# One GpSimd queue for loads and stores, with the last load behind the first store, in a rotary embedding kernel

## The chip, the cores and the metric

The kernel runs on one core of a Trainium2 chip. The metric is device time in microseconds (us). A profiled execution also gives a span, which is about 1.8 us shorter than the device time. All ratios are those of the same rounds on the same chip: the mean time of one kernel's fast runs over that of the other's. They are not quite the ratios of the medians, which are quoted beside them.

## The reference

```python
x: (8, 8, 1024, 64) float32, scale = 0.5
angles = np.outer(positions * scale, freqs)
cos, sin = np.cos(angles), np.sin(angles)
x_first, x_second = x[..., :32], x[..., 32:]
out_first  = x_first * cos - x_second * sin
out_second = x_first * sin + x_second * cos
return np.concatenate([out_first, out_second], axis=-1)
```

Each element is read once and written once: 16.8 MB in and 16.8 MB out, with little arithmetic.

## The kernel before

The 64 heads are cut into four units of 16. A unit is a tile of 128 partitions with 8192 elements each, 4.19 MB of float32 in memory. A load casts to fp16 on the way in; in this kernel all loads with a cast are issued by GpSimd. VectorE multiplies and adds in fp16. ScalarE casts the result to float32 in an output buffer, and a store brings it back. Half of unit 0 is loaded without a cast, by SyncE and ScalarE, so that work starts early.

```python
    xin = ctx.enter_context(tc.tile_pool(name="xin", bufs=1))     # one X tile for each unit
    xout = ctx.enter_context(tc.tile_pool(name="xout", bufs=3))   # output buffers (and X0f)
    ...
    pin(nc.gpsimd.dma_start(out=Xf[0][:, :NH], in_=xv[0][:, :NH]))
    ...                                        # small constants on GpSimd
    for u in range(1, NU):
        pin(nc.gpsimd.dma_start(out=Xf[u], in_=xv[u]))
    ...                                        # sine and cosine tables T
    for u in range(NU):
        OUT = xout.tile([P, N], FP32, tag="O")
        for s in range(2):
            ...                                # four VectorE instructions on half a unit
            pin(nc.scalar.copy(out=OUT[:, ns], in_=Xf[u][:, ns]))
            if u in (0, NU - 1):
                pin(nc.sync.dma_start(out=ov[u][:, ns], in_=OUT[:, ns]))
        if u not in (0, NU - 1):
            pin(nc.gpsimd.dma_start(out=ov[u], in_=OUT))
```

`pin` keeps program order on each engine. So GpSimd's queue (q0 in the profile) held X0 half, X1, X2, X3, S1, S2, and SyncE's queue (q1) held S0a, S0b, S3a, S3b after a first load. X is a load, S a store, the figure is the unit, and a and b are its halves.

Of the kernel before, what the change touches and what calls it, by code (L numbers as in the profile page):

```python
# [21 lines left out]
def kernel(  # L22
# [8 lines left out]
    nc = tc.nc  # L31
    pin = tc.keep_in_program_order
# [9 lines left out]
    NU = NBH // HEADS  # L42
# [9 lines left out]
    xv = x.rearrange("b h s d -> (b h s d)").rearrange("(u p n) -> u p n", p=P, n=N)  # L52
    ov = out.rearrange("b h s d -> (b h s d)").rearrange("(u p n) -> u p n", p=P, n=N)
# [21 lines left out]
    Xf = [t.rearrange("p k h j -> p (k h j)") for t in X]  # L75
# [12 lines left out]
        out=one, in_=one, compare_op=ALU.not_equal, fill=1.0, base=0,  # L88
        pattern=[[-1, G], [-G, HP]], channel_multiplier=1,
    ))  # L90
    for u in range(1, NU):
        pin(nc.gpsimd.dma_start(out=Xf[u], in_=xv[u]))  # L92


# [6 lines left out]
        out=posf, in_=pos_i64.bitcast(I32).rearrange("p (k t) -> p k t", t=2)[:, :, 0]  # L101
# [3 lines left out]
        out=y,  # L105
# [8 lines left out]
        out=r, in0=m, scalar=_MAGIC, in1=y, op0=ALU.subtract, op1=ALU.subtract  # L114
# [5 lines left out]
        out=ra.bitcast(I32), in0=r.bitcast(I32), scalar1=0x7FFFFFFF, scalar2=None, op0=ALU.bitwise_and  # L120
# [5 lines left out]
    for g in range(0, G, 2):  # L126
        ps = spread.tile([P, 2, 2, W], FP32, tag="g")
        for i in range(2):
            nc.tensor.matmul(  # L129
                out=ps[:, i].rearrange("p t w -> p (t w)"),  # L130
# [9 lines left out]
    pin(nc.scalar.copy(out=Xf[0][:, NH:], in_=X0f[:, :NH]))  # L140


    for u in range(NU):
        OUT = xout.tile([P, N], FP32, tag="O")
        for s in range(2):
            ks = slice(s * KH, (s + 1) * KH)
            ns = slice(s * NH, (s + 1) * NH)
            Xs = X[u][:, ks]
            sin_b = T[:, 0, ks].unsqueeze(2).broadcast_to((P, KH, 2, half))
            cos_b = T[:, 1, ks].unsqueeze(2).broadcast_to((P, KH, 2, half))  # L150
            pr = tmp.tile([P, KH, 2, half], FP16, tag="pr")
            pin(nc.vector.tensor_tensor(out=pr, in0=Xs, in1=sin_b, op=ALU.mult))  # L152
            pin(nc.vector.tensor_tensor(out=Xs, in0=Xs, in1=cos_b, op=ALU.mult))  # L153
            pin(nc.vector.tensor_tensor(  # L154
                out=Xs[:, :, 0, :], in0=Xs[:, :, 0, :], in1=pr[:, :, 1, :], op=ALU.subtract
            ))
            pin(nc.vector.tensor_tensor(  # L157
                out=Xs[:, :, 1, :], in0=pr[:, :, 0, :], in1=Xs[:, :, 1, :], op=ALU.add
            ))
            pin(nc.scalar.copy(out=OUT[:, ns], in_=Xf[u][:, ns]))  # L160
            if u in (0, NU - 1):
                pin(nc.sync.dma_start(out=ov[u][:, ns], in_=OUT[:, ns]))
        if u not in (0, NU - 1):
            pin(nc.gpsimd.dma_start(out=ov[u], in_=OUT))  # L164
# [33 lines left out]
```

## Time and profile before

| | before |
|---|---|
| device time, median of 3 runs | 84.39 us (84.28 to 84.39) |
| span of the profiled run | 82.5 us |
| VectorE busy | 60.3 us, without a pause from 13.07 to 69.53 us |
| last store issued | 73.2 us |
| transfer engines, mean busy share from 1.7 to 81.3 us | 1.00 |
| moved in memory | 16.79 MB read, 16.78 MB written |

Two rows of the table are the ones to look at, that of VectorE and that of the transfer engines. VectorE is the busiest engine, but it ends 13 us before the span does. The 16 transfer engines ("DMA" in the profile) are never idle between the first load and the last store.

The DMA view of a stretch lists for each queue the packets, the MB and the busy share of the 16 engines. A packet of more than a few bytes is one row, that is, one partition's part of one transfer. The windows view gives for a stretch its bounds and length, then the busy time of PE, PEld, VectorE, ScalarE and GpSimd with instruction counts, the clock granted to TensorE, the DMA share and the GB/s. A cast load is counted there at its fp16 size, half of what it reads. Both views count a packet, with its whole time and all its bytes, in the stretch in which it starts, so that a share can come out a little above 1.

### The profile page before, as it was taken

The numbers are of one execution on the slowest core, as the hardware profiler recorded it, in microseconds if no ns is written. First come the engines' busy times: TensorE is split into PE (matmuls) and PEld (weight loads), VectorE is DVE, ScalarE is ACT, GpSimd is POOL, SyncE is SP. The second block draws the span as 40 slices with busy tenths as digits, with TensorE's granted clock in tenths as the row PEclk, the third lists the DMA queues.
The fourth block names the chain that finished last, engine by engine and source line by source line (L and its number), as shares of the span: only waits on it lengthen the run. The fifth ranks groups of instructions, "written<-read, shape, count | busy, mean of one in ns | idle before, by whom it ended". The sixth has DMA issues, their size and how long they took to land.

```text
span 82.5 us, 179 instructions
## 1 busy us (share of the span) xinstructions
PE 7.1 (9%) x18; PEld 2.8 (3%) x18; DVE 60.3 (73%) x40; ACT 40.1 (49%) x18; POOL 4.6 (6%) x14
## 2 busy tenths in 40 slices
PE   0020999200000000000000000000000000000000
PEld 0020333000000000000000000000000000000000
DVE  0306476999999999999999999999999997000000
ACT  0603069999950790393098059219606902940000
POOL 4920000000000000000000200000200000000000
PEclk9999999985555555555555555555555555555555
DMA  2899998997996999799979999996998999799990
GB/s 48 336 319 278 290 326 187 254 246 159 230 254 127 254 262 342 270 278 350 278 191 302 270 342 421 461 524 286 508 509 350 413 508 461 302 445 429 397 485 24
DMA packets 1874, 26.22 MB, mean 318 GB/s; under 512 B 338, under 2 KB 338, under 8 KB 338
## 3 DMA queue, kind: packets, MB, share of 16 engines
q0 software_dynamic: 864, 15.73, 66.2%
q1 hardware_dynamic: 720, 9.44, 27.5%
q10 hardware_dynamic: 290, 1.06, 3.3%
HBM read 16.79 MB, written 16.78 MB: 407 GB/s over the span
## 4 chain that ended last, share of the span: by engine, by line
DVE 55%; ACT 15%; issue 6%; DMA 5%; PE 5%; DVEq 1%; ACTq 0%
DVE X L153 20%; DVE pr L152 20%; DVE X L157 9%; DVE X L154 6%; DMA freq_row<-in_freqs_dram 5%; ACT T L139 5%; ACT OUT L160 4%; PE ps L129 4%; ACT X L140 4%; DVEq L193 1%; PE cfreq L97 1%; ACT tab L122 1%; DVE r L113 1%; DVE y L104 1%; ACTq L69 0%
## 5 line engine op out<-in xcount | busy, mean ns | idle before, releaser
L160 ACT CAST OUT<-X 128x4096 f32<-128x4096 f16 x8 | 28.9, 3607 | 24.2 <-DVE X L157 24.2
L152 DVE TENSOR_TENSOR pr<-X,T 128x4096 f16<-128x4096 f16 x8 | 18.3, 2292 | 1.0 <-ACT T L139 0.7
L153 DVE TENSOR_TENSOR X<-X,T 128x4096 f16<-128x4096 f16 x8 | 18.3, 2292 | 0.3
L154 DVE TENSOR_TENSOR X<-X,pr 128x2048 f16<-128x2048 f16 x8 | 9.8, 1225 | 0.3
L157 DVE TENSOR_TENSOR X<-pr,X 128x2048 f16<-128x2048 f16 x8 | 9.7, 1218 | 0.0
L139 ACT CAST T<-ps 128x1024 f16<-128x1024 f32 x6 | 5.7, 1028 | 2.6 <-PE ps L129 2.6
L129 PE MATMUL ps<-tab,sel 128*128 128x512 f16 x16 | 6.5, 599 | 2.2 <-ACT tab L122 2.2
L164 POOL DMA_DIRECT2D out_dram<-OUT x2 | 1.1, 538 | 54.1 <-ACT OUT L160 54.1
L137 DVE CAST T<-ps 128x1024 f16<-128x1024 f32 x2 | 2.5, 1225 | 2.2 <-PE ps L129 2.2
L140 ACT CAST X<-X0f 128x4096 f16<-128x4096 f32 x1 | 3.6, 3649 | 0.0
L95 DVE COPY sel<-one 128x2048 f16<-128x2048 f16 x1 | 0.7, 693 | 2.8 <-POOL one L87 2.8
L129 PEld LDWEIGHTS <-sel 128*128 128x128 f16 x16 | 2.3, 143 | 6.1 <-issue 6.1
L117 ACT ACTIVATE tab<-r 128x256 f16<-128x256 f32 x1 | 0.4, 418 | 4.1 <-DVE r L113 4.1
L117 ACT ACT_TABLE_LOAD x1 | 1.3, 1283 | 2.1 <-issue 2.1
L92 POOL DMA_DIRECT2D X<-in_x_dram x3 | 2.0, 658 | 0.0
L100 DVE CAST posf<-pos_i 128x8 f32<-128x8 int32 x1 | 0.2, 172 | 2.3 <-DMA pos_i<-in_positions_dram 2.3
L97 PE MATMUL cfreq<-freq_row,coef 1*128 1x32 f32 x2 | 0.6, 392 | 5.6 <-DMA freq_row<-in_freqs_dram 5.6
L83 POOL DMA_DIRECT2D X<-in_x_dram x1 | 0.7, 669 | 0.8 <-POOLq L179 0.8
L97 PEld LDWEIGHTS cfreq<-freq_row,coef 1*128 1x128 f32 x2 | 0.5, 306 | 5.6 <-issue 5.6
L104 DVE TENSOR_TENSOR y<-posf,cfreq 128x256 f32<-128x256 f32 x1 | 0.4, 422 | 0.3 <-PE cfreq L97 0.3
L122 ACT ACTIVATE tab<-ra,quarter 128x256 f16<-128x256 f32 x1 | 0.5, 507 | 0.0
L113 DVE SCALAR_TENSOR_TENSOR r<-m,y 128x256 f32<-128x256 f32 x1 | 0.4, 424 | 0.0
(10 smaller groups left out, 1.9 us busy)
## 6 DMA issues: line engine op xcount, KB each, us to landing
out_dram<-OUT SPq DMA_DIRECT2D x4, 2048.0 KB, 14.8
out_dram<-OUT POOLq DMA_DIRECT2D x2, 4096.0 KB, 15.3
X<-in_x_dram POOLq DMA_DIRECT2D x3, 2048.0 KB, 31.9
X0f<-in_x_dram SPq DMA_DIRECT2D x1, 1024.0 KB, 4.8
X<-in_x_dram POOLq DMA_DIRECT2D x1, 1024.0 KB, 11.7
X0f<-in_x_dram ACTq DMA_DIRECT2D x1, 1024.0 KB, 13.2
pos_i<-in_positions_dram ACTq DMA_DIRECT2D x1, 8.0 KB, 5.0
freq_row<-in_freqs_dram ACTq DMA_DIRECT2D x1, 0.1 KB
```

Source lines behind the costliest of these rows:

```text
L92: pin(nc.gpsimd.dma_start(out=Xf[u], in_=xv[u]))
L97: nc.tensor.matmul(out=cfreq, lhsT=coef, rhs=freq_row, start=True, stop=True)
L117: pin(nc.scalar.activation(out=tab[:, 0], in_=r, func=AF.Sin, bias=0.0, scale=-_TWO_PI_DN))
L129: nc.tensor.matmul(out=ps[:, i].rearrange("p t w -> p (t w)"), lhsT=sel[:, g + i].rearrange("s h q -> s (h q)"), rhs=tab.rearrange("s t k ...
L137: pin(nc.vector.tensor_copy(out=dst, in_=ps))
L139: pin(nc.scalar.copy(out=dst, in_=ps))
L140: pin(nc.scalar.copy(out=Xf[0][:, NH:], in_=X0f[:, :NH]))
L152: pin(nc.vector.tensor_tensor(out=pr, in0=Xs, in1=sin_b, op=ALU.mult))
L153: pin(nc.vector.tensor_tensor(out=Xs, in0=Xs, in1=cos_b, op=ALU.mult))
L154: pin(nc.vector.tensor_tensor(out=Xs[:, :, 0, :], in0=Xs[:, :, 0, :], in1=pr[:, :, 1, :], op=ALU.subtract))
L157: pin(nc.vector.tensor_tensor(out=Xs[:, :, 1, :], in0=pr[:, :, 0, :], in1=Xs[:, :, 1, :], op=ALU.add))
L160: pin(nc.scalar.copy(out=OUT[:, ns], in_=Xf[u][:, ns]))
```

## The change

The intent is to keep loads and stores apart and to bring each load no earlier than it is needed. All loads with a cast and the stores S0a, S0b, S1 and S2 go through one queue, in the order X0 half, X1, X2, S0a, X3, S0b, S1, S2. Only unit 3's stores stay on SyncE.

```diff
-    for u in range(1, NU):
+    for u in range(1, NU - 1):
         pin(nc.gpsimd.dma_start(out=Xf[u], in_=xv[u]))
 ...
             pin(nc.scalar.copy(out=OUT[:, ns], in_=Xf[u][:, ns]))
+            eng = nc.sync if u == NU - 1 else nc.gpsimd
             if u in (0, NU - 1):
-                pin(nc.sync.dma_start(out=ov[u][:, ns], in_=OUT[:, ns]))
+                pin(eng.dma_start(out=ov[u][:, ns], in_=OUT[:, ns]))
+            if (u, s) == (0, 0):
+                pin(eng.dma_start(out=Xf[NU - 1], in_=xv[NU - 1]))
```

## The prediction

> **What bounds the kernel now.** I write X0 to X3 for the loads of the four units and S0 to S3 for their stores; S0a and S0b are the two halves of a unit's store, and "X0 half" is the half of unit 0 that GpSimd loads. Every full unit is 4.19 MB in memory. I first read the page's busy line and the compute part of the timeline.
>
> ```profile
> PE 7.1 (9%) x18; PEld 2.8 (3%) x18; DVE 60.3 (73%) x40; ACT 40.1 (49%) x18; POOL 4.6 (6%) x14
> ```
> ```profile
> 13.07 2.29 DVE L152 TENSOR_TENSOR pr<-X,T 128x4096 f16<-128x4096 f16 x1 [0.67 <-ACT T L139]
> ...
> 45.27 0.54 POOL L164 DMA_DIRECT2D out_dram<-OUT  x1 [40.60 <-ACT OUT L160]
> ...
> 55.47 2.29 DVE L152 TENSOR_TENSOR pr<-X,T 128x4096 f16<-128x4096 f16 x1
> ...
> 59.37 0.53 POOL L164 DMA_DIRECT2D out_dram<-OUT  x1 [13.55 <-ACT OUT L160]
> ...
> 68.31 1.22 DVE L157 TENSOR_TENSOR X<-pr,X 128x2048 f16<-128x2048 f16 x1
> 69.56 3.61 ACT L160 CAST OUT<-X 128x4096 f32<-128x4096 f16 x1 [3.40 <-DVE X L157]
> ```
>
> The columns of the second fence are start, duration, engine, line, operation, and in brackets the idle time before it. VectorE runs from 13.07 to 69.53 us: eight halves at 2.29 + 2.29 + 1.22 + 1.22 us plus small gaps, near 7.05 us each. None of the idle time before its multiplies is put down to a load. ScalarE's last cast ends at 73.17 us and S3b, the last store, is issued then. That chain is fixed by the multiplies. The page's chain of waits ends with that cast and hides what follows: 9.3 us from 73.17 to the end of the 82.5 us span. So I next asked for the DMA share in three stretches (last two columns: DMA share and GB/s), and for the queues.
>
> ```profile
> 0.00:1.70 1.70, 0.00 (x0) 0.00 (x0) 0.00 (x0) 0.00 (x0) 0.65 (x5) 1.00 0.00 0
> 1.70:81.30 79.60, 7.14 (x18) 2.78 (x18) 60.31 (x40) 40.14 (x18) 3.98 (x10) 0.60 1.00 329
> 81.30:82.50 1.20, 0.00 (x0) 0.00 (x0) 0.00 (x0) 0.00 (x0) 0.00 (x0) 0.50 0.00 0
> ```
> ```profile
> q0 software_dynamic: 864, 15.73, 66.2%
> q1 hardware_dynamic: 720, 9.44, 27.5%
> q10 hardware_dynamic: 290, 1.06, 3.3%
> HBM read 16.79 MB, written 16.78 MB: 407 GB/s over the span
> ```
>
> This is the reading that matters: between 1.7 and 81.3 us the share is 1.00, so the transfer engines never run dry. The three queues are busy 66.2 + 27.5 + 3.3 = 97.0% of 82.5 us = 80.0 us, and 33.57 MB in 79.6 us is 422 GB/s. GB/s in the windows is lower because a load is counted at its fp16 size. The kernel is bound by transfers from end to end; the chain of multiplies is only just hidden behind them.
>
> Then I took the price of a row (one partition of one transfer), with the DMA view in short windows. Here the columns are packets, MB, share of 16 engines.
>
> Loads only, 15 to 22.6 us:
> ```profile
> q0 software_dynamic: 113, 1.59, 98.2%
> ```
> Loads beside S0, 35.5 to 50.1 us:
> ```profile
> q0 software_dynamic: 143, 2.26, 66.7%
> q1 hardware_dynamic: 144, 2.10, 34.3%
> ```
> Stores only, 73.5 to 82.5 us:
> ```profile
> q1 hardware_dynamic: 224, 3.15, 81.7%
> ```
>
> Each transfer adds 16 tiny completion packets, which I take off. Load row: 0.982 x 7.6 x 16 / (113 - 16) = 1.23 us. Beside stores: 0.667 x 14.6 x 16 / 127 = 1.23 us, and a half-unit store row 0.343 x 14.6 x 16 / 128 = 0.626 us. Store row alone: 0.817 x 9 x 16 / (224 - 32) = 0.613 us. Between 59.5 and 66 us, S2 alone, the same division gives 1.214 us for a full-unit row. So a load row costs the same with or without stores beside it, and a store row gains 2% from being alone. The one dear stretch is the first meeting of loads and stores, 24.5 to 35.5 us: there a load row comes out at 1.34 us (114 packets, 74.6%), or 0.11 x 98 / 16 = 0.7 us lost per engine.
>
> **What the Trainium skill says.** "DMA: Bandwidth & Descriptors", section "Issuing engines are not separate DMA queues", says that transfers from all issuing engines end up on the same 16 DMA engines and interleave. The trace agrees: 66.7% + 34.3% makes 101% in the mixed stretch. Section "Queues, rings and completion order" says an engine takes turns between its queues packet by packet; with rows twice as long on one side that gives the load about two thirds of the time, and 66.7 to 34.3 is that. Section "Specifications" gives about 1 us to the first byte on the GpSimd path and 0.6 us on the SyncE path; no transfer of the trace before shows the first alone. "SBUF — State Buffer", section "SBUF: two separate sides", warns that VectorE in a two-port mode can hold up GpSimd's descriptor writing. The two GpSimd stores contradict it for these multiplies: both were issued amid them in 0.54 us, some 0.3 us after ScalarE's cast.
>
> **The change, part by part.** No instruction of VectorE, ScalarE or TensorE changes; the listing of the changed program shows the same sequence. GpSimd gets two issues more (at some 0.54 us each, on an engine 6% busy), SyncE two fewer. Bytes and rows stay the same. What moves is order: X2 no longer shares with S0a, and X3 no longer shares with S0a and S0b; X3 is issued at about 24.8 instead of 4.1 us, still long before the engines reach it.
>
> Landings before are issue time plus the DMA view's time to landing: X1 2.7 + 19.9 = 22.6; X2 35.5; X3 4.1 + 46.0 = 50.1; S0a 23.75 + 18.9 = 42.7; S0b 31.0 + 26.4 = 57.4; S1 45.3 + 16.9 = 62.2; S2 59.4 + 13.7 = 73.1; S3a 76.8; S3b 73.2 + 8.4 = 81.6. With one queue I add eight rows per engine and transfer, starting from X1 at 22.6:
> X2 8 x 1.23 -> 32.4; S0a 8 x 0.613 -> 37.3; X3 -> 47.2; S0b -> 52.1; S1 8 x 1.214 -> 61.8; S2 -> 71.5; S3a -> 76.4; S3b -> 81.3.
>
> The end moves by 0.3 us. If neighbouring rows overlap slightly, as a share just above 1 suggests, the 0.7 us meeting cost and 16 x 0.013 = 0.2 us for store rows could be recovered in full, some 0.9 us. What limits it: S2 cannot be issued before the cast that ends at 59.08 us, its issue ends at 59.9, and with a first byte about 1 us later (the skill's figure, so an estimate) its rows begin near 60.9. The queue now runs out of S1 rows just about there (60.9 to 61.5, landing less about 0.4). Gain beyond half a microsecond is then turned into a gap before S2. I choose 0.4 us: 84.39 - 0.4 = 84.0.
>
> Nothing else waits: VectorE needs X2 at 41.37 and X3 at 55.47 us; they come at 32.4 and 47.2. Unit 3's cast at 62.56 us reuses unit 0's output buffer, free at 52.1 instead of 57.4. These margins grow but are worth nothing, as none was a wait before.
>
> **The rivals.**
> 1. One queue is worse at handover: an engine stalls at each change from load to store because no second queue fills in. For: three more such changes (X2 to S0a, S0a to X3, X3 to S0b) and the unexplained 0.7 us when they first meet. Against: in the mixed stretch the engines alternate row by row at no extra cost. At 0.5 us each it makes 85.0 us or so.
> 2. The gap before S2 is long, because GpSimd's first byte is slower than estimated or because the queue gets there sooner. Each us of it beyond the saving is added to the end; 84.5 to 85.
> 3. Earlier X3 and freed buffers speed the chain up. Against: VectorE has no wait on either. Even if transfers had no backlog, S3b is issued at 73.2 and needs 8 x 0.613 = 4.9 us, about 0.4 us to landing and a first byte: 79.1 us at the very least, against 81.6; that floor is 81.9 us, and would need 2.5 us less transfer work that the change does not remove.
>
> **Range and chances.** The best plausible case is the full 0.9 us with a little more (83.3); the worst plausible case is a handover or gap of about 0.5 us net (84.9). The runs before spread by 0.1 us. Faster by over 2% means under 82.7 us, which needs 1.7 us of transfer time gone: 3%. Slower by over 2% means above 86.1: 3%.
>
> **What would show it.** DMA share still 1.00 from 1.7 to about 81 us; the new order of landings near 32, 37, 47 and 52 us; VectorE still from 13.07 to 69.5; no load row at 1.34 us around 25 us. A window around 60 to 61.5 us with a share below 1 would show the gap before S2. The prediction is wrong if the share drops below 1 anywhere else, if VectorE waits for X2 or X3, or if store rows from GpSimd cost more than the 0.613 us of those from SyncE.

## The result, and the profile after

The changed kernel took 84.57 us (median of 6 runs, 84.51 to 84.73); the kernel before took 84.39 us in the same rounds (84.08 to 84.67). The ratio is 1.0028, with a 95% interval of 1.0005 to 1.0051. So the change costs 0.24 us (0.0028 x 84.39): within 2%, but on the other side from the predicted gain of 0.4 us.

The page after, for the lines on queues, and the windows view of the changed kernel:

```profile
q0 software_dynamic: 1152, 19.92, 78.3%
q1 hardware_dynamic: 432, 5.24, 15.3%
q10 hardware_dynamic: 290, 1.06, 3.2%
HBM read 16.79 MB, written 16.78 MB: 405 GB/s over the span
```
```profile
0.00:1.70 1.70, 0.00 (x0) 0.00 (x0) 0.00 (x0) 0.00 (x0) 0.65 (x5) 1.00 0.00 0
1.70:81.70 80.00, 6.83 (x18) 2.66 (x18) 60.30 (x40) 40.13 (x18) 5.05 (x12) 0.60 1.00 328
```

The same bytes now go mostly through q0. The share is still 1.00, for 80.0 us where it was 79.6. So nothing went idle: the engines were busy longer with the same bytes. (The share is a mean and could hide a gap. The packet records of the two traces show none: from 2.5 to 80.8 us at least 14 packets are in flight at every moment, and 16 or more nearly always.) VectorE's 60.3 us did not change, nor did the issue of the last store (73.3 us, before 73.2).

Landings, as issue time plus the DMA view's time to landing, show where the time came in:

| transfer | landed before | predicted after | landed after | after less predicted |
|---|---|---|---|---|
| X2 | 35.5 | 32.4 | 3.6 + 29.8 = 33.4 | 1.0 |
| S0a | 42.7 | 37.3 | 24.1 + 14.4 = 38.5 | 1.2 |
| X3 | 50.1 | 47.2 | 24.7 + 23.4 = 48.1 | 0.9 |
| S0b | 57.4 | 52.1 | 31.3 + 21.6 = 52.9 | 0.8 |
| S1 | 62.2 | 61.8 | 45.4 + 17.3 = 62.7 | 0.9 |
| S3b | 81.6 | 81.3 | 73.3 + 8.7 = 82.0 | 0.7 |

The new order came as foreseen. But X2 is a microsecond late on landing, and everything after it carries nearly that microsecond to the end. So the loss lies in the rows up to the landing of X2. Both traces can be cut at row boundaries there. A window of two load rows on each engine should take 2.4 us. First the kernel before, then the changed kernel, each with two ordinary load rows and then the two ahead of the first store:

```profile
20.50:22.95 2.45, 0.00 (x0) 0.00 (x0) 2.42 (x2) 2.45 (x1) 0.00 (x0) 0.50 1.01 214
25.40:28.40 3.00, 0.00 (x0) 0.00 (x0) 2.96 (x3) 1.06 (x1) 0.00 (x0) 0.50 1.02 175
```
```profile
26.65:29.05 2.40, 0.00 (x0) 0.00 (x0) 2.37 (x2) 1.61 (x1) 0.00 (x0) 0.50 1.02 218
29.05:32.50 3.45, 0.00 (x0) 0.00 (x0) 3.38 (x3) 1.99 (x1) 0.54 (x1) 0.50 1.04 152
32.50:37.40 4.90, 0.00 (x0) 0.00 (x0) 4.83 (x4) 2.98 (x1) 0.00 (x0) 0.50 1.00 428
37.40:47.05 9.65, 0.00 (x0) 0.00 (x0) 9.51 (x6) 4.24 (x2) 0.54 (x1) 0.50 1.02 217
44.65:47.05 2.40, 0.00 (x0) 0.00 (x0) 2.37 (x2) 0.43 (x1) 0.54 (x1) 0.50 1.04 218
47.05:51.95 4.90, 0.00 (x0) 0.00 (x0) 4.83 (x4) 3.43 (x1) 0.00 (x0) 0.50 1.00 425
```

The last two columns carry it. In each of the two-row windows length times GB/s is 0.52 MB, that is 32 rows of 16 KB, two for each engine; only the time differs. Before, the two rows ahead of the first store took 3.00 us, 0.58 us more than the 2.42 us of two ordinary rows (9.65 us for the eight rows of X3 makes 1.21 us a row). After, they took 3.45 us, 1.03 us more. The share stays near 1: the engines count as busy while they move 152 in place of 218 GB/s, so an idle time would never show this. All else is as planned: S0a takes 4.90 us, X3 9.65, S0b 4.90. And the second change from load to store, X3 to S0b at 47.05, costs nothing visible: 2.40 us for the two rows ahead of it. I call the loss ahead of the first store the **handover loss** below and give it as the window of two rows less 2.42 us. It follows the leading engine at the window's ends, so engines that trail can lose more. Length times share gives the time of the rows themselves, as a mean of the 16 engines: 3.00 x 1.02 = 3.06 us before and 3.45 x 1.04 = 3.59 us after, so 0.5 us more on average, where the leading engine lost 0.45 us more.

### The profile page after: what moved, and what is told of

It is laid out like the page before. It is cut to its first block, busy times and chain, and to the rows that moved or that the text cites. A ratio compares the mean times of both kernels' runs of the same rounds, so it can differ in the third digit from the quotient of the medians.

```text
span 82.9 us, 179 instructions
## 1 busy us (share of the span) xinstructions
PE 6.8 (8%) x18; PEld 2.7 (3%) x18; DVE 60.3 (73%) x40; ACT 40.1 (48%) x18; POOL 5.7 (7%) x16
## 4 chain that ended last, share of the span: by engine, by line
DVE 55%; ACT 14%; issue 6%; DMA 5%; PE 5%; DVEq 1%; ACTq 0%
DVE pr L153 19%; DVE X L154 19%; DVE X L158 9%; DVE X L155 6%; DMA freq_row<-in_freqs_dram 5%; ACT T L139 5%; ACT OUT L161 4%; PE ps L129 4%; ACT X L140 4%; DVEq L197 1%; PE cfreq L97 1%; ACT tab L122 1%; DVE r L113 1%; DVE y L104 1%; ACTq L69 0%
## 5 line engine op out<-in xcount | busy, mean ns | idle before, releaser
L168 POOL DMA_DIRECT2D out_dram<-OUT x2 | 1.1, 536 | 27.1 <-ACT OUT L161 27.1
L164 POOL DMA_DIRECT2D out_dram<-OUT x2 | 1.1, 538 | 26.1 <-ACT OUT L161 26.1
## 6 DMA issues: line engine op xcount, KB each, us to landing
X<-in_x_dram POOLq DMA_DIRECT2D x3, 2048.0 KB, 23.4
```

## The experiments

Each edit is against the kernel that is named. Times are medians; where a ratio is given, it is that to the kernel before in the same rounds.

### Queue and order apart

**order_only**: before, with X3 held back until S0a's data is cast, S0 still on SyncE.

```diff
-    for u in range(1, NU):
+    for u in range(1, NU - 1):
 ...
                 pin(nc.sync.dma_start(out=ov[u][:, ns], in_=OUT[:, ns]))
+            if (u, s) == (0, 0):
+                late = consts.tile([P, 1], FP32)
+                pin(nc.gpsimd.tensor_copy(out=late, in_=OUT[:, 0:1]))
+                pin(nc.gpsimd.dma_start(out=Xf[NU - 1], in_=xv[NU - 1]))
```

> S0 stays on SyncE's queue, X3 is still issued only after the first half of unit 0 is cast (a tiny GpSimd copy out of that buffer, some 0.1 to 0.3 us, holds GpSimd until then). Theory A (the loss of the change is the stall of the load rows just ahead of the first store, and it is worse when the store sits in the same queue as the loads): the two rows before the first store lose about 0.6 us as in the kernel before, and the time is that of before, 84.3 to 84.5. Theory B (moving X3 late costs): the time is that of the changed kernel, 84.57, or more.

Measured: 84.19 us, ratio 0.9996 (0.9971 to 1.0020). The two rows ahead of S0a took 3.20 us, a handover loss of 0.78 us. So issuing X3 late costs nothing (theory B falls).

**queue_only**: before, with S0 on GpSimd's queue behind all loads.

```diff
+                eng = nc.sync if u == NU - 1 else nc.gpsimd
-                pin(nc.sync.dma_start(out=ov[u][:, ns], in_=OUT[:, ns]))
+                pin(eng.dma_start(out=ov[u][:, ns], in_=OUT[:, ns]))
```

> All four loads first, then S0, S1, S2 on GpSimd's one queue; only one change from load to store, at about 41.5 us. Theory A (stall at the first store of the program, wherever it comes in that queue): the last two load rows of X3 lose about 1.1 us together, nothing else does, time about 84.6. Theory C (each change from load to store in a queue costs, and the changed kernel has two): the same single loss, so no difference there, but if the loss depended on the time of day in the span (around 29 to 33 us) it would be at 29 to 33 us here too, or gone: 83.5.

Measured: 84.64 us, ratio 1.0048 (1.0024 to 1.0073). The windows view of its last loads and its first stores:

```profile
33.90:38.70 4.80, 0.00 (x0) 0.00 (x0) 4.73 (x3) 3.60 (x1) 0.00 (x0) 0.50 1.02 218
38.70:42.15 3.45, 0.00 (x0) 0.00 (x0) 3.38 (x4) 0.69 (x1) 0.00 (x0) 0.50 1.02 152
42.15:47.05 4.90, 0.00 (x0) 0.00 (x0) 4.83 (x3) 2.92 (x1) 0.53 (x1) 0.50 1.00 428
```

The loss is the same 1.03 us, but at 38.7 instead of 29 us. It goes with the first store, not with a moment in the span, and moving the stores to GpSimd's queue brings the whole cost of the change without the new order.

### Is it the first write to memory?

**before_warm** and **after_warm**: each kernel with a tiny store at the head of GpSimd's queue, overwritten later by unit 3's result.

```diff
+    wt = consts.tile([16, 128], FP32)
+    pin(nc.gpsimd.memset(wt, 0.0))
+    pin(nc.gpsimd.dma_start(out=ov[NU - 1][:16, :128], in_=wt))
     pin(nc.gpsimd.dma_start(out=Xf[0][:, :NH], in_=xv[0][:, :NH]))
```

> The kernel before plus a store of 16 x 512 bytes of zeros into a part of the output that is overwritten later, as the first transfer of GpSimd's queue. Theory A1 (the stall is a one-time cost of the first write to memory by each transfer engine): load rows at 25 to 29 us are 1.23 us again, and the time falls by up to 0.6 us to 83.8 unless the stall now shows in full at the start. Theory A2 (the stall comes from loads queued ahead of a store, not from a first write): no change at 25 to 29 us, time 84.4 or 0.1 us more.

> The changed kernel plus the same tiny early store. Theory A1: the last two load rows of X2 are 1.23 us, where they took 1.59 and 2.00 us; S0a starts about 1.1 us earlier; then the queue is early enough for a gap before S2 (issued at 59.5), so the time falls by 0.6 to 1.1 us to 83.5 to 84.0. Theory A2: the stall stays, time 84.6.

Measured: before_warm 85.40 us, ratio 1.0116 (1.0078 to 1.0153); after_warm 86.28 us, of which three runs were slow, ratio of the fast ones 1.0163 (1.0111 to 1.0216). The handover loss stayed: 0.78 us before S0a in the first (26.8 to 30.0 us), 1.33 in the second (28.85 to 32.6). Theory A1 falls, as far as a store of 512 bytes for each engine can test it; row_dram below writes a full row. That both became slower was not foreseen. The end of after_warm shows the form of it:

```profile
82.00:83.20 1.20, 0.00 (x0) 0.00 (x0) 0.00 (x0) 0.00 (x0) 0.00 (x0) 0.50 0.06 27
```

A share of 0.06 is what one engine of 16 makes (1/16), still storing while the others are done; in this run the others did not take over its rows, and the slowest engine set the end. Why the tiny store pushed some engines back was not followed further.

### Which side of the transfer?

**row_store**, **row_sbuf** and **row_dram**: the changed kernel with one 16 KB row for each engine between X1 and X2 in GpSimd's queue. The three differ in source and target; row_dram also has no memset, so that its chain of multiplies starts at 13.24 us, where it starts at 14.09 and 14.08 us in the other two.

```diff
     for u in range(1, NU - 1):
         pin(nc.gpsimd.dma_start(out=Xf[u], in_=xv[u]))
+        if u == 1:   # row_store and row_sbuf; row_dram has no memset
+            pin(nc.gpsimd.memset(X0f[:16, NH:], 0.0))
+            pin(nc.gpsimd.dma_start(out=ov[NU - 1][:16, :NH], in_=X0f[:16, NH:]))               # row_store
+            pin(nc.gpsimd.dma_start(out=X0f[16:32, NH:], in_=X0f[:16, NH:]))                    # row_sbuf
+            pin(nc.gpsimd.dma_start(out=ov[NU - 1][:16, :4096], in_=xv[NU - 1][:16, :4096]))    # row_dram
```

> The changed kernel with one 16 KB row per transfer engine of zeros stored (SBUF to memory) in GpSimd's queue between X1 and X2, into output that is overwritten later. Theory D (the stall is paid once, by the first full-sized store row of an engine): the last rows of X1, near 20 to 22 us, take about 1.1 us more in sum, and the last rows of X2 before S0a are 1.23 us each; time 84.6 + 0.6 = 85.2. Theory E (each first meeting with a long run of store rows costs, a single row is not enough): no or a small stall near 22 us and the full 1.1 us before S0a; time 85.2 to 86.3.

> The same with an SBUF to SBUF row of 16 KB per engine, so the source side is as in a store and memory isn't written. If the stall belongs to reading SBUF as a source for the first time: stall near 22 us, none before S0a. If it belongs to writing memory: none near 22 us, 1.1 us before S0a. Time about 85.2 either way.

> The same with a memory to memory row of 16 KB per engine, so memory is written but SBUF isn't read. If the stall belongs to writing memory for the first time at full rate: stall near 22 us, none before S0a. If it belongs to the SBUF source: the reverse.

| kernel | source and target of the row | time, ratio (95%) | two load rows ahead of the added row | two load rows ahead of S0a |
|---|---|---|---|---|
| row_store | SBUF to memory | 85.14, 1.0094 (1.0057 to 1.0131) | 2.60 us | 3.20 us |
| row_sbuf | SBUF to SBUF | 85.64, 1.0160 (1.0126 to 1.0194) | 2.65 us | 2.45 us |
| row_dram | memory to memory | 85.31, 1.0118 (1.0087 to 1.0148) | 2.40 us | 3.35 us |

The two rows ahead of S0a in row_store and in row_dram:

```profile
29.90:33.10 3.20, 0.00 (x0) 0.00 (x0) 3.13 (x3) 2.06 (x1) 0.54 (x1) 0.50 1.02 164
29.70:33.05 3.35, 0.00 (x0) 0.00 (x0) 3.28 (x3) 1.41 (x1) 0.54 (x1) 0.50 1.07 157
```

The lines of row_sbuf, the row itself with the first row of X2 behind it and then the two rows ahead of S0a:

```profile
22.05:24.95 2.90, 0.00 (x0) 0.00 (x0) 2.87 (x2) 2.69 (x1) 0.00 (x0) 0.50 1.09 181
31.00:33.45 2.45, 0.00 (x0) 0.00 (x0) 2.42 (x2) 0.95 (x1) 0.54 (x1) 0.50 1.00 214
```

In row_sbuf S0a pays nothing any more. A loss came at the added row instead: 0.23 us ahead of it, and the row with the first row of X2 took 2.90 us where 0.61 + 1.21 = 1.82 would be expected, if an SBUF to SBUF row cost what a store row costs (no run shows its undisturbed price). In row_dram, where memory is written but the source is memory too, S0a pays 0.93 us, about as if nothing had been there. So the loss is not that of the first full row written to memory. But SBUF as the source does not settle it either: the row of row_store has the same source as that of row_sbuf, and it took only 0.18 us and left 0.78 for S0a, which is between theories D and E. The two differ in their target alone, so what frees S0a is shown for a row from SBUF to SBUF and for nothing wider. All three kernels have higher ratios (1.0094 to 1.0160) than the changed kernel (1.0028).

**sbuf_small**: the changed kernel with an SBUF to SBUF transfer of 2 KB for each engine on ScalarE's queue amid the loads.

```diff
+    wt = consts.tile([16, 512], FP32)
+    wt2 = consts.tile([16, 512], FP32)
 ...
+    pin(nc.gpsimd.memset(wt, 0.0))
 ...
+    pin(nc.scalar.dma_start(out=wt2, in_=wt))
     pin(nc.scalar.copy(out=Xf[0][:, NH:], in_=X0f[:, :NH]))
```

> The changed kernel with an SBUF to SBUF transfer of 2 KB per engine on ScalarE's queue in the middle of the loads (about 16 us). row_sbuf showed that a 16 KB SBUF row among the loads takes the stall on itself and frees S0a from it. If a 2 KB row does so more cheaply, the rows ahead of S0a are 1.23 us and the time is 83.6 to 84.2, under both kernels. If the stall scales with the bytes read ahead, S0a still pays nearly all of it: 84.6 to 84.8.

Measured: 84.67 us, ratio 1.0039 (1.0014 to 1.0064). The two rows ahead of S0a took 3.15 us, a loss of 0.73 us, so this small row doesn't free S0a. Other sizes between 2 and 16 KB were not tried.

### A store with no load ahead of it, and once or again

**drained**: the changed kernel with X2 issued after S0a, so that the queue runs dry ahead of S0a.

```diff
-    for u in range(1, NU - 1):
+    for u in range(1, NU - 2):
 ...
-                pin(eng.dma_start(out=Xf[NU - 1], in_=xv[NU - 1]))
+                for v in (NU - 2, NU - 1):
+                    pin(eng.dma_start(out=Xf[v], in_=xv[v]))
```

> X2 is issued only after S0a, so the engines run dry after X1 (landed at 22.6 us) until S0a is issued at 24.1 us: some 3 us idle, S0a with no load row ahead of it. Theory D (once, at the first store): S0a's first row or its start shows an extra 1 us, the later change from X3 to S0b costs under 0.1 us as in the changed kernel. Theory F (the cost comes from load rows in flight ahead of a store, at their first meeting): S0a's rows are 0.61 us from the start, and the last two rows of X3 before S0b now lose about 1.1 us. Time about 87 either way: 84.6 + 3 less what the stall no longer costs.

Measured: 88.71 us, ratio 1.0521 (1.0484 to 1.0557). The windows view of the idle stretch, of S0a, and of the two load rows ahead of S0b:

```profile
22.30:25.40 3.10, 0.00 (x0) 0.00 (x0) 3.03 (x3) 1.86 (x1) 0.94 (x2) 0.50 0.00 0
25.40:28.00 2.60, 0.00 (x0) 0.00 (x0) 2.57 (x3) 0.23 (x1) 0.65 (x2) 0.50 1.00 403
48.10:51.55 3.45, 0.00 (x0) 0.00 (x0) 3.38 (x3) 2.60 (x1) 0.00 (x0) 0.50 0.98 152
```

S0a ran at 403 GB/s from its start, so it shows no first cost near 1 us. (Its last three rows, ahead of X2, did take 2.50 us in place of 1.84, a loss at the change from store to load that the changed kernel doesn't have; drained_one below shows it too, 2.30 us from 28.25 to 30.55. It was not followed.) Now the two rows of X3 ahead of S0b paid 1.03 us, a handover that was free in the changed kernel. That fits theory F: the loss goes with the first store that stands behind loads in flight. But it could also mean that any long run of loads brings it back: 16 load rows lie between S0a and S0b in drained, 8 in the changed kernel. Three more looks were asked for to tell these apart (one profile each, not timed in rounds).

**row_sbuf_early** (row_sbuf with its row ahead of X1), **drained_one** (drained with X3 behind S0b) and **row_sbuf_again** (row_sbuf unchanged).

```diff
+    pin(nc.gpsimd.memset(X0f[:16, NH:], 0.0))                                   # row_sbuf_early, against after
+    pin(nc.gpsimd.dma_start(out=X0f[16:32, NH:], in_=X0f[:16, NH:]))
     for u in range(1, NU - 1):
 ...
-            if (u, s) == (0, 0):                                                # drained_one, against after
-                pin(eng.dma_start(out=Xf[NU - 1], in_=xv[NU - 1]))
+            if u == 0:                                                          # and range(1, NU - 2) as in drained
+                pin(eng.dma_start(out=Xf[NU - 2 + s], in_=xv[NU - 2 + s]))
```

> row_sbuf with the SBUF row put ahead of X1 in the queue, at about 12 us, so 16 load rows per engine lie between it and S0a where row_sbuf had 8. Theory K (the loss comes once per program, at the first SBUF source behind loads): the two load rows ahead of S0a lose nothing (2.4 us for the two, as in row_sbuf). Theory H (the loss comes back after a long run of loads; 8 rows are too few, 16 are enough): they lose 0.7 to 1.1 us (3.1 to 3.5 us for the two).

> drained with only X2 between S0a and S0b (8 load rows per engine instead of 16), X3 after S0b. Theory K (once, at the first store that stands behind loads): the last two rows of X2 before S0b lose 0.9 to 1.1 us as X3's did in drained. Theory H: 8 rows are too few, no loss there (2.4 us for the two); then X3 and S1, again 8 load rows, none either. Time near 88 either way, as the idle stretch stays.

> row_sbuf once more: that its SBUF row frees S0a rests on one profile. If it holds, the last two rows of X2 take 2.4 to 2.5 us together again; if it was chance, 3.1 to 3.5 us.

Measured, in this order, 85.67, 88.70 and 85.39 us in one run each. The two rows ahead of S0a in row_sbuf_early:

```profile
31.00:33.45 2.45, 0.00 (x0) 0.00 (x0) 2.42 (x2) 0.81 (x1) 0.54 (x1) 0.50 1.00 214
```

The two rows ahead of S0b in drained_one:

```profile
37.90:41.50 3.60, 0.00 (x0) 0.00 (x0) 3.40 (x3) 0.16 (x2) 0.00 (x0) 0.50 0.99 146
```

Sixteen load rows after an SBUF row brought no loss back, and eight load rows ahead of the first store with loads before it were enough for 1.18 us, so H falls. Theory K fits these cases as far as "once" goes: after the loss has been paid, a later store behind loads is free, X3 to S0b in the changed kernel and X3 to S1 in drained_one (2.40 us for the two rows from 53.60 to 56.00). Its other half, that the first SBUF source behind loads pays, does not fit row_store, where such a row paid 0.18 us and S0a behind it 0.78. And as both drained kernels also lose time at S0a to X2, they leave open whether that change, or the idle stretch, set something back. row_sbuf_again repeated its 2.45 us.

### Which half of the change brings it, and does it repeat?

**after_again** is the changed kernel once more. **s0b_pool** is before with S0b alone moved to GpSimd; **s0a_pool** is the changed kernel with S0b alone moved back to SyncE.

```diff
+                eng = nc.gpsimd if (u, s) == (0, 1) else nc.sync       # s0b_pool, against before
-                pin(nc.sync.dma_start(out=ov[u][:, ns], in_=OUT[:, ns]))
+                pin(eng.dma_start(out=ov[u][:, ns], in_=OUT[:, ns]))
 ...
-            eng = nc.sync if u == NU - 1 else nc.gpsimd                # s0a_pool, against after
+            eng = nc.gpsimd if (u, s) == (0, 0) else nc.sync
```

> The changed kernel once more, in the same rounds as the next three. Theory G (the change wins 0.2 to 0.3 us by keeping loads and stores apart and loses some 0.5 us because its first store, queued behind loads in the same queue, stalls the two rows ahead of it by 1.1 us in place of 0.6): ratio 1.002 to 1.004 to the kernel before, the two rows ahead of S0a at about 1.6 and 2.0 us. If the stall was an accident of one run, it isn't here.

> The kernel before with only S0b moved to GpSimd's queue (behind X3); S0a stays on SyncE's. Theory G: the stall is the two-queue one, 0.6 to 0.7 us; eight rows fewer are mixed, which is worth 8 x 0.013 = 0.1 us; time 84.2 to 84.3, 0.0 to 0.2 us under before. Rival (the number of stores on GpSimd's queue is what costs): half way to the changed kernel, 84.5.

> The changed kernel with only S0b back on SyncE's queue, beside X3. Theory G: the stall is the one-queue one, 1.1 us ahead of S0a, and eight rows are mixed: 84.6 to 84.8, at or just above the changed kernel. Rival: half way to before, 84.45.

The two load rows ahead of S0a in order_only, s0b_pool (here with one row more, 33), after_again and s0a_pool:

```profile
25.40:28.60 3.20, 0.00 (x0) 0.00 (x0) 3.17 (x3) 1.15 (x1) 0.08 (x1) 0.50 0.99 164
25.50:28.40 2.90, 0.00 (x0) 0.00 (x0) 2.87 (x3) 1.09 (x1) 0.00 (x0) 0.50 1.05 186
29.05:32.35 3.30, 0.00 (x0) 0.00 (x0) 3.23 (x3) 2.22 (x1) 0.54 (x1) 0.50 1.04 159
29.10:32.40 3.30, 0.00 (x0) 0.00 (x0) 3.23 (x3) 1.94 (x1) 0.00 (x0) 0.50 1.02 159
```

The kernels without added transfers, by the queue of S0a (handover loss from one profile each):

| kernel | S0a on | handover loss | median, us | ratio to before (95%) |
|---|---|---|---|---|
| before | SyncE | 0.58 | 84.3 to 84.4 | 1 |
| order_only | SyncE | 0.78 | 84.19 | 0.9996 (0.9971 to 1.0020) |
| s0b_pool | SyncE | 0.48 | 84.44 | 1.0007 (0.9979 to 1.0034) |
| changed kernel | GpSimd | 1.03 | 84.57 | 1.0028 (1.0005 to 1.0051) |
| after_again | GpSimd | 0.88 | 84.77 | 1.0049 (1.0022 to 1.0075) |
| queue_only | GpSimd | 1.03 | 84.64 | 1.0048 (1.0024 to 1.0073) |
| s0a_pool | GpSimd | 0.88 | 84.56 | 1.0025 (1.0001 to 1.0049) |

The column "S0a on" splits both others without an overlap: losses of 0.48 to 0.78 us with ratios around 1, against 0.88 to 1.03 us with ratios of 1.0025 to 1.0049. (The intervals of single kernels overlap; the split rests on all seven together.) Where S0b goes makes no difference that these runs can see. So the cost of the change comes from one transfer: S0a in the queue that already holds the loads. Whether it is the shared queue that costs, or that S0a is on GpSimd's kind of queue (software_dynamic in the profile) and not on SyncE's, these runs can't tell: no run has S0a on GpSimd's queue and the loads on another. On average the loss grows from 0.61 to 0.96 us, by 0.34 us, while a saving of at most 0.2 us on mixed rows stands against it. The measured cost of 0.24 us (0.41 in after_again, 0.0049 x 84.28) is of that size.

The profiled pair can be closed from its packet records. Summed over the trace and divided by 16 engines, the 16 KB load rows take 0.50 us more after the change and the 16 KB store rows 0.11 us less; with small rests all packets together take 80.53 us in place of 80.10. That is the 0.4 us in the last landing. The same sum is 80.10 to 80.20 us in the three kernels with S0a on SyncE and 80.34 to 80.53 us in the four with S0a on GpSimd.

No kernel beats the kernel before beyond its interval.

## Why the prediction was right or wrong

- **The bound**: right. Transfer engines busy from 1.7 us to the end in both kernels, VectorE's chain unchanged, no wait on X2 or X3. That is why a new order could move the time only by the price of a row.
- **The prices and the order**: right. S0a 4.90 us, X3 9.65, S0b 4.90 are the predicted 8 x 0.613, 8 x 1.23 and 8 x 0.613 within 0.2 us. Store rows from GpSimd cost no more than those from SyncE. Load rows sit 1.21 us apart, slightly overlapped, as the prediction allowed.
- **The step that failed** is the prediction's "the 0.7 us meeting cost and 16 x 0.013 = 0.2 us for store rows could be recovered in full", and with it the sum that put X2 at 32.4 us. The meeting cost was seen in the trace and its size was right. But it was left unexplained, and treated as a cost that ends when loads and stores no longer *share* the engines, which a single queue would bring about. The runs show that it comes with the first store behind loads in flight, whichever of the two queues holds it, and that it is larger, 0.88 to 1.03 in place of 0.48 to 0.78 us, when that store stands in the loads' own queue. So the term of -0.7 us at best became +0.34 us on average. The other term, 0.2 us for store rows, did come in part: 0.11 us in the profiled pair. What the prediction made of the sum, -0.4 us, became +0.24.
- **Rival 1** (a single queue stalls at each handover) was right about the place and wrong about the count. It was argued away because "in the mixed stretch the engines alternate row by row at no extra cost". That is true, but the mixed stretch lies after the loss has been paid. Of the three new changes between load and store only the first cost anything.
- **Rival 2** (a gap before S2) did not come. The queue reached S2 late enough: the landing of S1 at 62.7 is after the issue of S2 at 59.5, and the packet records show 16 packets in flight all through the stretch around it, 59 to 66 us. GpSimd's first byte itself, about 1 us in the Trainium skill's "DMA: Bandwidth & Descriptors", section "Specifications", agrees: in drained, where the queue had run dry, the issue of S0a began at 24.46 us and the share is 0.00 up to 25.4 us and 1.00 from there.
- **Rival 3** (a faster chain) did not come, for the reason given.
- **A reading that went too far**: the two GpSimd stores do not contradict the warning about VectorE that the prediction quotes. The warning is about a two-port mode, and no line shows that these multiplies use one; and the 0.54 us are the time of the issue, not that of writing descriptors. Nothing in the sum rests on it.
- **Within 2%** was right, and the range held; the direction was wrong.

What is shown: with the engines busy throughout, the loss falls on the load rows just ahead of the first store, once, and it is larger with that store on GpSimd's queue. What stays open is why: what happens inside a transfer engine there, why a row from SBUF to SBUF frees the later store and a row from SBUF to memory hardly does, and whether the shared queue or the kind of queue makes the loss larger.

## What to carry to other kernels

When transfers bind and the engines are busy throughout, read the price of a row in each stretch (GB/s at a share of 1.00), not the idle time: a stretch at 152 instead of 218 GB/s looks just as busy. If such a stretch has no explained cause, a prediction shouldn't count on the change to remove it: find out first what it goes with. Reordering transfers without removing bytes was worth between nothing and a loss of 0.5% here, and 5% where it let the engines run dry (drained).

## What the Trainium skill lacked or had wrong

- "DMA: Bandwidth & Descriptors" has nothing on the handover loss: with loads from memory in flight, the first store cost the two load rows ahead of it 0.48 to 0.78 us when it came from SyncE's queue and 0.88 to 1.03 us from GpSimd's, which also held the loads (1.18 in drained_one); later stores behind loads cost nothing visible. A full SBUF to SBUF row of 16 KB among the loads freed the later store (2.45 us for the two rows); 2 KB did not (3.15 us).
- The same page, section "Issuing engines are not separate DMA queues", says that starting transfers on several engines only saves the time of the issue. Here the choice of engine also moved the handover loss by about 0.3 us, or 0.3 to 0.5% of the kernel's time.
- The same page, section "Queues, rings and completion order", says that an engine drains a whole packet, some 9 to 17 descriptors, from one queue before it turns to the next. How long a newly issued transfer waits for its first turn it doesn't say. SyncE's first store in the kernel before was issued at 23.75 us, and from 23.7 to 28.4 us the DMA view lists 48 packets on q0 and none on q1: its first row began some 4.7 us after the issue. From then on the queues alternate row by row: 16 packets on q1 from 28.4 to 29.0 us, 16 on q0 to 30.2, 16 on q1 to 30.8.
